# Layer A of a two-layer decoder step: scores by groups of chunks, odd units' scores and substitution beside the running chain

## The chip, the cores and the metric

One core of one Trainium2 chip runs the whole step as one program. The metric is device microseconds of one execution, the median of several. Five engines work side by side, each through its own list of instructions in a fixed order: PE (matmuls), DVE and ACT (elementwise work), POOL (a little elementwise work) and SP (which issues the DMAs). An instruction that waits holds up everything behind it on its engine.

## The reference, cut to what matters

Layer 0 is RWKV-7 time mixing over 272 prompt positions (16 meta tokens and 256 prompt tokens), 64 heads of 64; layer 1 is sliding-window attention. The change touches the recurrence of layer 0:

```python
def rwkv7_step(S, inp):
    r, d, k, v, kk, b = inp
    sa = jnp.einsum('bhij,bhj->bhi', S, kk)
    S = S * d[:, :, None, :] - sa[..., None] * b[:, :, None, :] + v[..., None] * k[:, :, None, :]
    return S, jnp.einsum('bhij,bhj->bhi', S, r)
...
rkvz = jnp.einsum('btpd,pde->btpe', xm[:, :, :4], w_rkvz)
S_fin, y = lax.scan(rwkv7_step, S0.astype(f32), (tm(r_h), tm(d_h), tm(k_h), tm(v_h), tm(kk), tm(b_h)))
...
return y @ w_out, S_fin.astype(S0.dtype), xn[:, -1]
```

## The kernel before, in words

**Big products.** Every large product is made with weights split into a high and a low part: `wunits` (L200) loads 256 KB of weights as one unit, ACT casts the high part `whi` (L195), DVE subtracts to get the low part `wlo` (L197), and PE makes three matmuls for each (L218 to L220). The pool that holds `raw`, `whi` and `wlo` has 5 buffers of each, so the split of unit u+5 can begin only when PE is done with unit u. A unit is 12 matmuls in two pieces of 6; the name of a unit ends with its place along the contraction, in steps of 2 (`wlo_v_1536_0`, `wlo_v_1536_2` follow each other, and after `_14` comes `_0` of the next column block).

**Phase A.** `drive` (L611) runs the products of layer 0 as the backbone: one piece per turn, counted by `self.pos`, and between pieces it lets generators ("streams") write their own instructions. A stream's `yield n, need` says: not before n more pieces, and not before the condition `need`. `after(n, *ks)` is the condition that the marks ks were set at least n pieces ago. PE's order is exactly the order in which this is written. DVE's and ACT's order is made by a scheduler by priority and expected times; the streams in `now` (epilogues and main) are written without a tie to the weights, main with a priority raised by 2000, and all others are tied behind the last split but one.

**The recurrence.** Heads go in 16 units u of four heads, in pairs o of an even and an odd unit. A unit is prepared by `prep` (decays, normalised keys) and `prep_e` (the tiles `KB`, keys times decay, and `E`, scored operands, one tile for all 272 positions). `scores` (L1000) then makes, by chunks of 64 positions (four, and one of 16), the products between positions (L1017, L1031), masks them back into `E` (L1024, L1025, L1037, L1038), and at its end transposes the keys to `BK` (L1049). After the odd unit's scores, `substitute` (L1054) inverts small triangular blocks on DVE: a transpose `NL` (L1069), 14 steps of two instructions (L1075, L1077), and the transposes `TN` and `TR` (L1081, L1082). `solve` (L1092) puts the blocks together on PE: `ps_so` (L1102) reads `TN`, and three more rounds follow (L1108, L1120, L1129). `chain` (L1170) then walks the five chunks; each step is three groups of matmuls (L1191, L1205 with L1208, L1214 with L1217) with copies on ACT and DVE between them, spaced 5, 2 and 3 pieces. `group_norm` (L1257) normalises and turns the result back (`ps_yt`, L1275).

In `main` these follow each other for each pair: chain of o, then scores of the next odd unit, substitution, solve of o+1, chain of o+1. The even unit's scores run beside the chain as a side stream. From the turn in which `substitute` is written to the first `ps_so` there are 3 and 3 pieces of the transposes and then 24 (27 from the sixth pair on): 30 or 33 pieces.

Of the kernel before, what the change touches and what calls it, by code (L numbers as in the profile page):

```python
# [109 lines left out]
class Kernel:  # L110
# [467 lines left out]
    def phase_a(self):  # L578
# [15 lines left out]
        for a in (self.KB, self.F, self.N16, self.Noff, self.Y):  # L594
# [9 lines left out]
        self.drive(self.products(), [self.epilogues(), self.main(), preps, self.decodes(), self.late_gates(), self.keep_r()],  # L604
                   {preps: [wait, need]})
# [4 lines left out]
    def drive(self, products, streams, begun, ahead=2000):  # L610
# [3 lines left out]
        now = streams[:2]  # L614
# [49 lines left out]
    def main(self):  # L664
        for o in range(-1, NU // 2):
            n = 2 * o + 2
            if o >= 0:
                yield from self.chain(o)
                self.mark('u', o)
                self.side.append(self.group_norm(o))  # L670
            if n < NU:
                yield 0, self.after(0, ('p', n + 1), ('c', n))
                self.side.append(self.load_x(o + 1))
                self.prep_e(n + 1)
                self.mark('e', n + 1)
                yield from self.scores(n + 1)
                yield from self.solve(o + 1)

                self.samples = True
                self.mark('s', o + 1)  # L680

    def preps(self):
        for n in range(NU):
            if n % 2 == 0 and n:
                yield 0, self.after(0, ('e', n - 1))
# [4 lines left out]
            if n % 2 == 0:  # L690

                self.prep_e(n)
                self.side.append(self.even_scores(n))

    def even_scores(self, n):
        if n:
            yield 0, self.after(0, ('s', n // 2 - 1))
        yield from self.scores(n)
# [159 lines left out]
    def prep(self, u):  # L858
# [31 lines left out]
        kT = w("kT", 2)  # L890
# [34 lines left out]
        if u >= 4:  # L925
            yield 0, self.after(0, ('g', u // 2 - 2))
        vT = w("vT", 4)
        dma(vT, self.vd[b][:, sl])

        sm = rp.tile([128, 2, 6, NS], F32, tag="sm", name=f"sm{u}")  # L930
        for i, x in enumerate((kk, a, kT, rT, vT, Pp[:, :, 5:])):
# [16 lines left out]
        for j in range(2):  # L948
            rk_of(j)
        for j in range(2):  # L950
# [8 lines left out]
    def prep_e(self, u):  # L959

        nc, rp = self.nc, self.rp
        V, A, G = nc.vector, nc.scalar, nc.gpsimd
        tt = V.tensor_tensor
        MU = ALU.mult
        kT, rT, kk, a, cl = (self.U[u][n] for n in ('kT', 'rT', 'kk', 'a', 'cl'))
        Pp = self.Pp
        ch = lambda x: x[:, :, :256].rearrange("p q (c t) -> p q c t", t=64)
        pch = Pp[:, :, :260].rearrange("p q (c t) -> p q c t", t=65)
# [5 lines left out]
        A.copy(KB[64:128, :, :, 128:192], KB[64:128, :, :, 0:64])  # L974

        E = rp.tile([128, 5, 2, L], F32, tag="E", bufs=3, name=f"E_{u}")
        tt(ch(E[:, 0]), ch(kk), pch[:, :, :, 0:64], op=MU)
        tt(ch(E[:, 2]), ch(rT), pch[:, :, :, 1:65], op=MU)
        tt(E[:, 0, :, 256:272], kk[:, :, 256:272], Pp[:, :, 260:276], op=MU)
        tt(E[:, 2, :, 256:272], rT[:, :, 256:272], Pp[:, :, 261:277], op=MU)  # L980
        A.copy(E[64:128, 1], E[64:128, 0])
        self.U[u]['E'] = E

    def scores(self, u):
        nc, rp = self.nc, self.rp

        odd = u % 2
        gap = iter((8, 3, 4, 3, 3) if odd else (8, 6, 6, 5, 4))
        turn = iter((0, odd, 0, odd, 0))
        def banks(nm):  # L990
            if next(turn):
                two = self.two_banks(f"ps_{nm[0]}{nm[1]}")
                return [two[:, q] for q in range(2)]
            return [self.bank(self.pe, f"ps_{nm[0]}{q}{nm[1]}") for q in range(2)]
        V, A, G = nc.vector, nc.scalar, nc.gpsimd
        tt = V.tensor_tensor
        MU = ALU.mult
        KB, E = self.KB, self.U[u]['E']
        i0 = 8 * (u % 2)
        H = lambda q: slice(64 * q, 64 * q + 64)  # L1000
        BK = rp.tile([128, 2, 5, 128], F32, tag="BK", bufs=3, name=f"BK{u}")
        self.U[u].update(BK=BK)

        rows = lambda q, j, a, b: E[H(q), q:3:2 - q, j, a:b]
        inst = lambda a, r, cs: a[r, i0:i0 + 8].rearrange("p (a c) t -> p a c t", c=4)[:, :, cs]
        bc = lambda m, *s: m.unsqueeze(1).unsqueeze(1).to_broadcast(s)
        for c0 in (0, 2):
            cs = slice(c0, c0 + 2)
            yield next(gap)
            ps = [b.rearrange("p (a c t) -> p a c t", a=2, c=2) for b in banks(("sc", f"{c0}_{u}"))]  # L1010

            with self.pe_order():
                for j in range(2):
                    for c in range(2):
                        for q in (1, 0):
                            o = 64 * (c0 + c)
                            nc.tensor.matmul(ps[q][:, j, c], KB[H(q), j, c0 + c, 64 * q:64 * q + 128],  # L1017
                                             rows(q, j, o, o + 64), start=True, stop=True)
            for q in range(2):
                pv, kr = ps[q], H(1 - q)  # L1020
                out = lambda i, r: E[r, i, :, 64 * c0:64 * c0 + 128].rearrange("p a (c t) -> p a c t", c=2)
                for r, a, t0 in ((64 * q, self.F, 0), (64 * q + 32, self.ND, 32)):
                    A.copy(inst(a, slice(r ^ 64 * odd, (r ^ 64 * odd) + 32), cs), pv[r:r + 32, :, :, t0:64])
                tt(out(q, kr), pv[kr, :, :, 0:64], bc(self.cst(C_MASK, 64, kr), 64, 2, 2, 64), op=MU)  # L1024
                tt(out(3 + q, slice(0, 128)), pv[:, :, :, 64:128], bc(self.cst(C_MASK + 64, 64), 128, 2, 2, 64), op=MU)  # L1025
        yield next(gap)
        ps = [b[:, :64].rearrange("p (a h t) -> p a h t", a=2, h=2) for b in banks(("sc", f"4_{u}"))]
# [945 lines left out]
```

## Time and profile before

| What | Value |
|---|---|
| Median of 3 runs | 2115.6 us (2114.31 to 2118.69) |
| The profiled execution | 2118.32 us |
| Its span in the trace | 2116.5 us |
| Granted TensorE clock, mean | 0.99 |
| PE, DVE, ACT, POOL busy, share of the span | 98%, 80%, 60%, 6% |
| DMA | 446.28 MB, 211 GB/s over the span |

The profiled execution is 2.7 us above the median of the runs, and 1.8 us of it lie outside the span. A busy share of PE counts a matmul to its modelled end, so that PE is shown idle only where the next instruction came later than that. In views of waits, "PE ps_so L1102 <- DVE TN L1081" says that PE's instruction of line 1102 started when DVE had finished line 1081.

### The profile page before, as it was taken

Reading aid. Unit: us, or ns where it says so; the run is one execution under the profiler, and the core shown is the slowest. Engines: PE = TensorE matmul, PEld = TensorE weight load, DVE = VectorE, ACT = ScalarE, POOL = GpSimd, SP = SyncE. Lnnn points to the kernel's source line nnn. Section 1 sums busy time; section 2 is a strip of 40 time slices with the busy share of each in tenths; the row PEclk is TensorE's granted clock in tenths of the full one; section 3 lists DMA queues with packets and bytes.
Section 4 is the critical chain, followed back from the end, with each engine's and each line's share of the span. In section 5 each row is a group of like instructions: output and inputs, shape, how many; then the busy total and the mean of one; then the engine's idle time right before and its main releaser. Section 6 shows DMA issues by size and latency. Waiting matters only on the chain.

```text
span 2116.5 us, 55871 instructions
## 1 busy us (share of the span) xinstructions
PE 2064.9 (98%) x21420; PEld 1965.8 (93%) x21420; DVE 1697.8 (80%) x4112; ACT 1263.8 (60%) x2790; POOL 122.5 (6%) x188
## 2 busy tenths in 40 slices
PE   9999999899999999999999999999999999999997
PEld 7999899889899989899999999999999999999997
DVE  8867777687678878888888788997888888878885
ACT  3457766576766757767676445565565655544443
POOL 0011100001010010100100001100000000000000
PEclk9999999999999999999999999999999999999999
DMA  7898667658756876777657687757455444567774
GB/s 258 314 312 250 189 213 241 188 181 290 216 180 205 260 229 198 211 217 222 203 152 246 207 257 243 247 172 227 132 167 156 146 155 130 181 210 247 232 219 132
DMA packets 276356, 446.28 MB, mean 211 GB/s; under 512 B 54056, under 2 KB 97768, under 8 KB 275696
## 3 DMA queue, kind: packets, MB, share of 16 engines
q1 hardware_dynamic: 275656, 441.66, 66.6%
q8 instruction: 168, 2.75, 0.5%
q10 hardware_dynamic: 432, 1.05, 0.1%
q14 instruction: 100, 0.82, 0.1%
HBM read 381.69 MB, written 65.03 MB: 211 GB/s over the span
## 4 chain that ended last, share of the span: by engine, by line
PE 87%; DVE 5%; ACT 3%; DMA 3%; issue 2%; SPq 0%; POOL 0%; DVEq 0%; POOLq 0%; ACTq 0%
PE ps_z L218 6%; PE ps_z L219 6%; PE ps_z L220 6%; PE ps_k L218 3%; PE ps_ob L218 3%; PE ps_ob L220 3%; PE ps_v L218 3%; PE ps_ob L219 3%; PE ps_r L218 3%; PE ps_q L218 3%; PE ps_q L220 3%; PE ps_q L219 3%; PE ps_k L219 3%; PE ps_k L220 3%; PE ps_v L220 3%; PE ps_v L219 3%
## 5 line engine op out<-in xcount | busy, mean ns | idle before, releaser
L218 PE MATMUL ps_z<-mhlm,whi_z 128*128 128x280 f32 x512 | 158.6, 310 | 2.8 <-ACT sr L937 2.0
L219 PE MATMUL ps_z<-mhlm,whi_z 128*128 128x280 f32 x512 | 150.6, 294 | 0.0
L220 PE MATMUL ps_z<-mhlm,wlo_z 128*128 128x280 f32 x512 | 150.3, 294 | 0.0
L218 PE MATMUL ps_q<-bmh,whi_qb 128*128 128x264 f32 x512 | 150.0, 293 | 0.1
L218 PE MATMUL ps_z<-bmh,whi_zb 128*128 128x264 f32 x512 | 147.4, 288 | 0.0
L220 PE MATMUL ps_q<-bmh,wlo_qb 128*128 128x264 f32 x512 | 145.6, 284 | 0.6 <-DVE wlo_qb L197 0.6
L219 PE MATMUL ps_q<-bml,whi_qb 128*128 128x264 f32 x512 | 145.6, 284 | 0.0
L219 PE MATMUL ps_z<-bml,whi_zb 128*128 128x264 f32 x512 | 145.5, 284 | 0.0
L220 PE MATMUL ps_z<-bmh,wlo_zb 128*128 128x264 f32 x512 | 145.4, 284 | 0.0
L218 PE MATMUL ps_ob<-ghi,whi_ob 128*128 128x264 f32 x512 | 145.3, 285 | 0.0
L220 PE MATMUL ps_ob<-ghi,wlo_ob 128*128 128x264 f32 x512 | 144.6, 284 | 0.0
L219 PE MATMUL ps_ob<-glo,whi_ob 128*128 128x264 f32 x512 | 144.6, 283 | 0.0
L195 ACT CAST whi_ob<-raw_ob 128x512 fp32r<-128x512 f32 x128 | 79.1, 620 | 96.9 <-PE ps_ob L219 77.8
L195 ACT CAST whi_oa<-raw_oa 128x512 fp32r<-128x512 f32 x128 | 79.2, 620 | 88.0 <-PE ps_oa L219 30.6
L197 DVE TENSOR_TENSOR wlo_r<-raw_r,whi_r 128x512 fp32r<-128x512 f32 x128 | 87.8, 691 | 42.6 <-ACT whi_r L195 41.3
L218 PE MATMUL ps_v<-mhlm,whi_v 128*128 128x280 f32 x384 | 119.8, 312 | 0.4 <-ACT st L790 0.4
L218 PE MATMUL ps_k<-mhlm,whi_k 128*128 128x280 f32 x384 | 119.1, 310 | 1.0 <-ACT st L790 1.0
L195 ACT CAST whi_v<-raw_v 128x512 fp32r<-128x512 f32 x128 | 79.0, 619 | 65.8 <-PE ps_v L219 37.7
L197 DVE TENSOR_TENSOR wlo_v<-raw_v,whi_v 128x512 fp32r<-128x512 f32 x128 | 87.3, 687 | 36.9 <-ACT whi_v L195 35.6
L195 ACT CAST whi_zb<-raw_zb 128x512 fp32r<-128x512 f32 x128 | 78.2, 619 | 62.9 <-PE ps_z L219 38.5
L220 PE MATMUL ps_k<-mhlm,wlo_k 128*128 128x280 f32 x384 | 112.4, 293 | 2.1 <-issue 2.1
L219 PE MATMUL ps_v<-mhlm,whi_v 128*128 128x280 f32 x384 | 112.7, 293 | 0.0
(478 smaller groups left out, 7604.1 us busy)
## 6 DMA issues: line engine op xcount, KB each, us to landing
raw_k<-a_w_rkvz SPq DMA_DIRECT2D x128, 256.0 KB
raw_v<-a_w_rkvz SPq DMA_DIRECT2D x128, 256.0 KB
raw_r<-a_w_rkvz SPq DMA_DIRECT2D x128, 256.0 KB
raw_z<-a_w_rkvz SPq DMA_DIRECT2D x128, 256.0 KB
raw_oa<-a_w_out SPq DMA_DIRECT2D x128, 256.0 KB
raw_qb<-b_w_qz SPq DMA_DIRECT2D x128, 256.0 KB
raw_zb<-b_w_qz SPq DMA_DIRECT2D x128, 256.0 KB
raw_ob<-b_w_o SPq DMA_DIRECT2D x128, 256.0 KB
```

The source lines that it names most:

```text
L195: self.nc.scalar.copy(hi, src)
L197: return self.nc.vector.tensor_tensor(lo, src, hi.bitcast(F32), op=ALU.subtract)
L218: mm(ps, wh, xh, start=start, stop=False)
L219: mm(ps, wh, xl, start=False, stop=False)
L220: return mm(ps, wl, xh, start=False, stop=stop)
```

## The change

Scored operands are kept as three tiles for each unit (`E0` for chunks 0 and 1, `E1` for 2 and 3, `E2` for the last 16 positions) and the transposed keys as two (`BK0` for chunks 0 and 1, `BK1` for the rest). `prep_e` is cut into `prep_k` (the keys) and two parts; `scores` makes one group of chunks at a call; `turns` makes the transposes, those of chunks 0 and 1 together with the scores of the last chunk in one PSUM bank. `substitute` is cut into `strict` (its POOL part) and the rest, which uses `TN` as scratch in place of `stmp`. A new stream `odds` does the odd unit's work of pair o as soon as the chain of o-1 has finished chunk 1 (marks `k`), and `main` holds only chain and solve: the solve comes 24 pieces after the mark `t`, which is set where `substitute` is written. `odds` is in `now` but main alone keeps the raised priority. A chain step is spaced 6, 3 and 4 pieces. The four `TT` activations move from `substitute` into `solve`, behind the first `ps_so`. The chain's last chunk reads 64 columns of `E` where it read 16, and its memset and one copy of `W` are gone. `vT` is loaded later, `kT` has one buffer in place of two.

```diff
-        self.drive(self.products(), [self.epilogues(), self.main(), preps, self.decodes(), self.late_gates(), self.keep_r()],
-                   {preps: [wait, need]})
+        self.drive(self.products(), [self.epilogues(), self.main(), self.odds(), preps, self.decodes(), self.late_gates(),
+                                     self.keep_r()], {preps: [wait, need]}, now=3)
...
-        now = streams[:2]
+        now = streams[:now]
...
     def main(self):
         for o in range(-1, NU // 2):
-            n = 2 * o + 2
             if o >= 0:
                 yield from self.chain(o)
                 self.mark('u', o)
                 self.side.append(self.group_norm(o))
-            if n < NU:
-                yield 0, self.after(0, ('p', n + 1), ('c', n))
+            if 2 * o + 2 < NU:
                 self.side.append(self.load_x(o + 1))
-                self.prep_e(n + 1)
-                self.mark('e', n + 1)
-                yield from self.scores(n + 1)
+                yield 0, self.after(24, ('t', o + 1))
                 yield from self.solve(o + 1)
...
+    def odds(self):
+        for o in range(NU // 2):
+            u = 2 * o + 1
+            step = lambda c: [('k', o - 1, c)] if o else []
+            yield 0, self.after(0, ('p', u), ('c', u - 1), *step(1))
+            self.prep_k(u)
+            self.mark('b', u)
+            self.prep_e(u, 0)
+            yield 8
+            self.scores(u, 0)
+            yield 6
+            self.scores(u, 4)
+            yield 5, self.after(1, *step(3))
+            self.prep_e(u, 1)
+            self.mark('e', u)
+            yield 6
+            self.scores(u, 2)
+            self.strict(o)
+            yield 6
+            self.substitute(o)
+            self.mark('t', o)
+            yield 4, self.after(0, *([('u', o - 1)] if o else []))
+            self.turns(u, 1)
+            self.mark('c', u)
...
-        yield 24 if o < 5 else 27
+        TT = self.TT = rp.tile([128, 20, 64], F32, tag="TT", name=f"TT{o}")
         ps = self.bank(self.pe, f"ps_so{o}")
...
         ET = ev("ET", 16, 16)
         V.tensor_copy(ET, ps[:, 0:256].rearrange("p (i s) -> p i s", s=16))
+        for b in range(4):
+            A.activation(TT[:, :, 16 * b:16 * b + 16], TR[:, :, 0:20].rearrange("p t i -> p i t"), AF.Copy,
+                         scale=self.cst(C_M64 + 16 * b, 1))
...
-            yield (5 if c else 3), (None if c or not o else self.after(2, ('g', o - 1)))
+            yield (6 if c else 3), (None if c or not o else self.after(2, ('g', o - 1)))
...
-            yield 2
+            yield 3
...
-            yield 3
+            yield 4
...
-            yield 3 if j else 36 if o < NU // 2 - 1 else 19
+            yield 3 if j else 24 if o < NU // 2 - 1 else 19
```

What the change does to the order shows best where the second pair (o = 1) is solved. First DVE before; `NL1` and `stmp1` are the substitution's tiles, `wlo_v_1280_14` is the last unit of a column block and `wlo_v_1536_0` the first of the next:

```order
L1077 TENSOR_TENSOR NL1_5077<-NL1_5077,stmp1_14_5118 128x2x14
L197 TENSOR_TENSOR wlo_v_1280_14_5425<-raw_v_1280_14_5422,whi_v_1280_14_5424 128x512
L904 TENSOR_TENSOR kT4_5445<-kT4_5445,km1_4_5457 128x280
L906 TENSOR_TENSOR ta4_4872<-ta4_4872,kk4_5449 128x560
L1081 STREAM_TRANSPOSE TN1_5123<-NL1_5077 128x512
L1082 STREAM_TRANSPOSE TR1_5124<-NL1_5077 128x512
L1276 SCALAR_TENSOR_TENSOR vT0_2043<-ps_yt0_0_5399,par_79,vT0_2043 128x272
L197 TENSOR_TENSOR wlo_v_1536_0_5475<-raw_v_1536_0_5472,whi_v_1536_0_5474 128x512
```

`TN1` stands behind the split of unit `v_1280_14`. The same place on DVE now:

```order
L197 TENSOR_TENSOR wlo_v_1536_10_5665<-raw_v_1536_10_5662,whi_v_1536_10_5664 128x512
L974 SCALAR_TENSOR_TENSOR rk0_4_5775<-rT4_5452,par_79,kT4_5450 128x272
L974 SCALAR_TENSOR_TENSOR rk1_4_5779<-rT4_5452,par_79,kT4_5450 128x272
L1123 TENSOR_TENSOR TN1_5188<-NL1_5187 128x52
L1127 MEMSET NL1_5187 128x16 x2
L197 TENSOR_TENSOR rkllo4_5774<-rk0_4_5775,rklhi4_5773 128x272
L1125 TENSOR_TENSOR NL1_5187<-NL1_5187,TN1_5188 128x4x13
L197 TENSOR_TENSOR rkllo4_5774<-rk1_4_5779,rklhi4_5773 128x272
L1123 TENSOR_TENSOR TN1_5188<-NL1_5187 128x28
L1125 TENSOR_TENSOR NL1_5187<-NL1_5187,TN1_5188 128x2x14
L1128 STREAM_TRANSPOSE TN1_5188<-NL1_5187 128x512
L1129 STREAM_TRANSPOSE TR1_5189<-NL1_5187 128x512
```

`TN1` has moved behind the split of unit `v_1536_10`, and work of another unit (`rk`, `rkllo`) stands between the last steps of the substitution. On PE, the place of the first `ps_so1` before:

```order
L218 MATMUL ps_v_1280_1_5310<-mhlm2_11_7_5014,whi_v_1280_14_5424 128x280
L219 MATMUL ps_v_1280_1_5310<-mhlm2_11_7_5014,whi_v_1280_14_5424 128x280
L220 MATMUL ps_v_1280_1_5310<-mhlm2_11_7_5014,wlo_v_1280_14_5425 128x280
L218 MATMUL ps_v_1536_0_5518<-mhlm2_11_0_4747,whi_v_1536_0_5474 128x280
L219 MATMUL ps_v_1536_0_5518<-mhlm2_11_0_4747,whi_v_1536_0_5474 128x280
L220 MATMUL ps_v_1536_0_5518<-mhlm2_11_0_4747,wlo_v_1536_0_5475 128x280
L218 MATMUL ps_v_1536_0_5518<-mhlm2_11_0_4747,whi_v_1536_0_5474 128x280
L219 MATMUL ps_v_1536_0_5518<-mhlm2_11_0_4747,whi_v_1536_0_5474 128x280
L220 MATMUL ps_v_1536_0_5518<-mhlm2_11_0_4747,wlo_v_1536_0_5475 128x280
L1102 MATMUL ps_so1_5538<-TN1_5123,Noff_1742 32x16 x64
```

and now:

```order
L218 MATMUL ps_v_1536_1_5514<-mhlm2_11_0_4700,whi_v_1536_0_5440 128x280
L219 MATMUL ps_v_1536_1_5514<-mhlm2_11_0_4700,whi_v_1536_0_5440 128x280
L220 MATMUL ps_v_1536_1_5514<-mhlm2_11_0_4700,wlo_v_1536_0_5441 128x280
L218 MATMUL ps_v_1536_0_5513<-mhlm2_11_1_4718,whi_v_1536_2_5492 128x280
L219 MATMUL ps_v_1536_0_5513<-mhlm2_11_1_4718,whi_v_1536_2_5492 128x280
L220 MATMUL ps_v_1536_0_5513<-mhlm2_11_1_4718,wlo_v_1536_2_5493 128x280
L218 MATMUL ps_v_1536_0_5513<-mhlm2_11_1_4718,whi_v_1536_2_5492 128x280
L219 MATMUL ps_v_1536_0_5513<-mhlm2_11_1_4718,whi_v_1536_2_5492 128x280
L220 MATMUL ps_v_1536_0_5513<-mhlm2_11_1_4718,wlo_v_1536_2_5493 128x280
L883 MATMUL ps_vt10_0_5545<-consts_78,st2_10_5502 128x128 x2
L883 MATMUL ps_vt10_0_5545<-consts_78,st2_10_5502 16x128
L1145 MATMUL ps_so1_5552<-TN1_5188,Noff_1742 32x16 x64
```

Before, PE reached `ps_so1` in unit `v_1536_0`, one unit past the split in front of `TN1`. Now it reaches it in unit `v_1536_2`, four units short of the split in front of `TN1`, with 6 matmuls of a product and 3 transposes since the end of unit `v_1536_0`.

The same counts for all eight pairs, from the two orders: by how many units the last split in front of `TN` is ahead of the unit in which PE reaches the first `ps_so`; for the changed kernel also how many instructions DVE has from that split to `TN`, both included, and how many matmuls of products PE has from the end of the unit whose buffer that split takes to `ps_so`.

| Pair o | 0 | 1 | 2 | 3 | 4 | 5 | 6 | 7 |
|---|---|---|---|---|---|---|---|---|
| units ahead, before | 4 | -1 | 1 | 1 | 0 | 5 | 1 | -1 |
| units ahead, now | 4 | 4 | 3 | 4 | 4 | 4 | 4 | 3 |
| DVE instructions, now | 8 | 12 | 8 | 17 | 13 | 31 | 23 | 3 |
| matmuls between, now | 6 | 6 | 22 | 6 | 6 | 6 | 6 | 18 |

Three more counts from the orders. In phase A the places where PE has something else between two products were 368 and are 348. The first `kk` that is built from the second group's key norms (`kk4`) stood 4 weight splits behind the last step of those norms on DVE and now stands 7 behind. The last `ps_yt` of phase A stood 23 pieces ahead of the products' end and now stands 54 ahead.

More of the change, by code (lines that the diff above doesn't have):

```diff
@@ L974, in prep_e @@
         A.copy(KB[64:128, :, :, 128:192], KB[64:128, :, :, 0:64])
[L976 to L980, printed above, removed]
-        A.copy(E[64:128, 1], E[64:128, 0])
[L982 to L998, printed above, removed]
+        self.U[u]['E'], self.U[u]['BK'] = {}, {}
@@ L1019, in scores @@
             for q in range(2):
                 pv, kr = ps[q], H(1 - q)
[L1021 to L1025, printed above, removed]
@@ L1194, in chain @@
             W2 = W.rearrange("p (f k) i -> p f (k i)", f=2)
-            if c < 4:
-                A.copy(W2, part(0, slice(0, 128)))
-            else:
-                G.memset(W, 0.0)
-                for q in range(2):
-                    A.copy(W2[R(q)], part(0, R(q)))
-            yield 2
+            A.copy(W2, part(0, slice(0, 128)))
+            yield 3
             with self.pe_order():
```

194 lines of the change are left out of this document (121 added, 73 removed).

## The prediction, on record before the run

> **What bounds the kernel now.** I read the page's busy times first, then a table of busy times by stage, then the waits of PE in the stage that the change touches, then the timeline around the two largest of them.
>
> ```profile
> PE 2064.9 (98%) x21420; PEld 1965.8 (93%) x21420; DVE 1697.8 (80%) x4112; ACT 1263.8 (60%) x2790; POOL 122.5 (6%) x188
> ```
>
> PE bounds the whole. The table has, for a stretch in us, its length, then busy time (and instructions) of PE, PEld, DVE, ACT and POOL, then PE's granted clock, DMA share and GB/s; phase A is the first row.
>
> ```profile
> 200.00:1215.00 1015.00, 983.92 (x12721) 922.45 (x12719) 806.41 (x1834) 682.32 (x1523) 79.04 (x124) 0.98 0.69 214
> 1215.00:2000.00 785.00, 782.38 (x6554) 764.91 (x6553) 659.98 (x1816) 430.47 (x978) 23.49 (x28) 1.00 0.63 193
> ```
>
> PE idles 1015.00 - 983.92 = 31.1 us in phase A and 2.6 behind it. So nothing but phase A can give or take time, and that the last chain now ends earlier is worth nothing by itself. The largest waits there (us in total, times, longest):
>
> ```profile
> PE ps_yt L1275 <- DVE vT L1276: 8.0, 2, 6.9
> PE ps_so L1102 <- DVE TN L1081: 6.1, 2, 3.5
> ...
> PE ps_z L218 <- ACT sr L937: 2.0, 1, 2.0
> ```
>
> The second row is the solve waiting for the substitution: two of eight solves. This is the first of them, pair 0 (start, duration):
>
> ```profile
> 252.14 0.69 DVE L197 TENSOR_TENSOR wlo_r<-raw_r,whi_r 128x512 fp32r<-128x512 f32 x1 [0.17 <-ACT whi_r L195]
> 252.46 0.29 PE L220 MATMUL ps_r<-mhld,wlo_r 128*128 128x280 f32 x1
> 252.75 0.92 DVE L898 SCALAR_TENSOR_TENSOR kk<-kT,par,kk 128x280 f32<-128x280 f32 x2
> 253.69 1.33 DVE L910 TENSOR_TENSOR_SCAN cl<-reset,cl 128x272 f32<-128x272 f32 x2
> 255.14 1.05 DVE L1081 STREAM_TRANSPOSE TN<-NL 128x512 f32<-128x512 f32 x1
> 256.24 0.44 PE L1102 MATMUL ps_so<-TN,Noff 32*32 32x16 f32 x31 [3.50 <-DVE TN L1081]
> ```
>
> And pair 5:
>
> ```profile
> 911.42 0.69 DVE L197 TENSOR_TENSOR wlo_z<-raw_z,whi_z 128x512 fp32r<-128x512 f32 x1
> 912.03 0.18 DVE L1077 TENSOR_TENSOR NL<-NL,stmp 128x28 f32<-128x28 f32 x1
> 912.25 1.04 DVE L1081 STREAM_TRANSPOSE TN<-NL 128x512 f32<-128x512 f32 x1
> 913.43 0.78 PE L1102 MATMUL ps_so<-TN,Noff 32*32 32x16 f32 x43 [2.56 <-DVE TN L1081]
> ```
>
> DVE had no way to be earlier: the split in front of TN waits for a buffer that PE frees only at the end of the unit before the one in which it reaches the solve, since the buffers are five deep and the split is 4 (pair 0) and 5 (pair 5) units ahead. PE then runs out of work while DVE goes from that split to TN. In the other six pairs the split is at most one unit ahead, and none of them waits. Let S be the sum of DVE's work from that split to TN, both included. For pair 0 it is 4.6 (the rows shown and two small steps between them) and the wait 3.50, with 9 matmuls between freed buffer and solve; for pair 5 it is 2.0 and the wait 2.56, with none. So a wait is S - 1.1 with nine matmuls and S + 0.6 with none; for six, in proportion, S - 0.5.
>
> **The change, part by part.** *The solve's wait.* Now that split is 3 or 4 units ahead in every pair: the lag from the substitution to the solve is 24 pieces instead of 30 or 33, and the substitution's steps, without main's priority, are mixed with other DVE work. The durations (group, count, busy us, mean ns, idle before):
>
> ```profile
> L197 DVE TENSOR_TENSOR wlo_v<-raw_v,whi_v 128x512 fp32r<-128x512 f32 x96 | 65.5, 687 | 29.7 <-ACT whi_v L195 28.4 <-DMA vt<-vk 0.8
> L794 DVE SCALAR_TENSOR_TENSOR st<-th,st 128x280 f32<-128x280 f32 x32 | 14.2, 443 | 1.0 <-ACT th L793 1.0
> L945 DVE SCALAR_TENSOR_TENSOR rk<-rT,par,kT 128x272 f32<-128x272 f32 x29 | 13.3, 495 | 0.0
> L1266 DVE TENSOR_TENSOR Y<-Y,gvar 128x1536 f32<-128x1536 f32 x7 | 12.3, 1751 | 0.1
> L197 DVE TENSOR_TENSOR rkllo<-rk,rklhi 128x272 fp32r<-128x272 f32 x30 | 12.2, 433 | 0.5 <-ACT rklhi L195 0.4
> L1081 DVE STREAM_TRANSPOSE TN<-NL 128x512 f32<-128x512 f32 x8 | 8.8, 1096 | 0.1
> L806 DVE SCALAR_TENSOR_TENSOR st<-st,yl 128x544 f32<-128x544 f32 x12 | 8.6, 718 | 0.0
> L1077 DVE TENSOR_TENSOR NL<-NL,stmp 128x88 f32<-128x88 f32 x16 | 4.0, 248 | 0.3
> L1077 DVE TENSOR_TENSOR NL<-NL,stmp 128x28 f32<-128x28 f32 x16 | 3.1, 192 | 0.2
> ```
>
> Pair 1 has 12 instructions: split 0.69, two `rk` 0.99, two `rkllo` 0.87, four last steps 0.8, two memsets 0.15 (estimated under the smallest step), TN 1.10: S = 4.6, wait 4.1. Pair 5 has 31: split 0.69, one instruction like L794 0.44, two like L806 1.44, `Y` 1.75, seventeen steps of the substitution at 0.25 4.2, TN 1.10, and eight small ones at 0.1 to 0.19 each: S = 10.4 to 11.1, taken 10.8, wait 10.3. By the same rows pairs 0, 3, 4 and 6 have S = 4.4, 5.5, 4.0 and 8.5, waits 3.9, 5.0, 3.5, 8.0. Pairs 2 and 7 have S = 2.7 and 2.0 and some twenty matmuls between: 0.4 and 0.2. Together 35.4 where 6.1 stands now: +29.3. Bounds: with 0.6 more or less for each of the six, +25.5 to +33.
>
> *The clock behind a wait.* Stretches behind the waits at 256, 382, 913 and 1049 us:
>
> ```profile
> 257.50:260.90 3.40, 3.40 (x16) 3.40 (x16) 0.87 (x2) 2.92 (x5) 0.00 (x0) 0.50 0.22 33
> 382.00:387.10 5.10, 5.10 (x23) 5.09 (x24) 2.21 (x4) 3.44 (x6) 0.00 (x0) 0.50 0.49 165
> 913.50:919.60 6.10, 6.10 (x146) 6.03 (x147) 1.26 (x3) 3.96 (x6) 0.20 (x1) 0.50 0.85 278
> 1049.40:1052.70 3.30, 3.30 (x16) 3.30 (x15) 2.79 (x7) 1.09 (x2) 0.00 (x0) 0.50 0.55 153
> ```
>
> PE ran at half clock for 3.3 to 6.1 us, so each cost half of that: 1.7, 2.6, 3.1 and 1.6. The two behind `ps_so` cost 4.8 now. Six waits of 3.5 us or more at 2.5 each make 15: +10.2, between 6 x 1.6 - 4.8 = +4.8 and 6 x 3.1 - 4.8 = +13.8. The Trainium skill ("TensorE: Matmul & The Clock Gate", Part 1: The HAM clock gate) lets the clock fall only after an idle window of about 3.4 us; the rows show half clock also behind 2.56 and 2.0 us, so the trace differs. By that rule the same six waits count and the two small ones don't, so that the sum would hardly move.
>
> *The key norms.* The 6.9 us wait at `ps_yt` comes from DVE, which stood still for this:
>
> ```profile
> 375.65 0.51 DVE L898 SCALAR_TENSOR_TENSOR kk<-kT,par,kk 128x280 f32<-128x280 f32 x1 [4.24 <-DMA kk<-kr]
> ```
>
> That `kk` now stands seven splits behind the norms where it stood four. PE needs a new split every 12 matmuls, and matmuls follow each other 0.13 us apart (below), 1.55 us a unit: three more units are 4.65, over 4.24. So 6.9 and its 2.6 of clock go: -9.5, or nothing if the load starts later by as much.
>
> *Other waits.* 31.1 - 6.1 - 6.9 = 18.1 us of idle time in many waits of 2 us and less, and three stretches of half clock (the one at 1049 among them) of 1.6 each: 22.9. The chain's steps are 13 pieces where they were 10, so their products wait less often, and every wait for TN lets DVE and ACT catch up. I let half go, -11.4; the ends are 0 and -22.9.
>
> *Changes between products and other matmuls.* 20 fewer.
>
> ```profile
> 536.51 0.29 PE L220 MATMUL ps_k<-mhlm,wlo_k 128*128 128x280 f32 x1
> 536.74 1.20 PE L1120 MATMUL ps_so<-TN,F 32*32 32x32 f32 x64
> ...
> 537.87 0.40 PE L218 MATMUL ps_k<-mhlm,whi_k 128*128 128x280 f32 x1
> 538.10 0.29 PE L219 MATMUL ps_k<-mhlm,whi_k 128*128 128x280 f32 x1
> 538.23 0.29 PE L220 MATMUL ps_k<-mhlm,wlo_k 128*128 128x280 f32 x1
> ```
>
> Going in takes 0.23 where products follow each other after 0.13, and so does coming back: 0.2 each, -4 (0 if the groups joined paid nothing).
>
> *The last chunk* reads 64 columns where it read 16:
>
> ```profile
> L1191 PE MATMUL ps_ch<-X,E 128*64 128x64 f32 x368 | 16.3, 229 | 1.4 <-DVE X L1227 1.1 <-ACT X L1227 0.2
> L1191 PE MATMUL ps_ch<-X,E 128*16 128x64 f32 x112 | 4.4, 220 | 0.0
> ```
>
> 112 x 9 ns = +1.0. The memset and the copy that go, the group cuts of `E`, and the four `TT` activations behind the first `ps_so` are taken at nothing: DVE and ACT are idle for 209 and 333 us of phase A, and pieces of products lie between the solve's rounds. If that cover is gone they show as a wait at the solve's later rounds.
>
> Sum: +29.3 +10.2 -9.5 -11.4 -4.0 +1.0 = +15.6. On the profiled execution 2118.3 + 15.6 = 2133.9; that execution is 2.7 above the median, so 2131 us (+0.7%).
>
> **The rivals.**
> (a) *The waits for TN grow.* A stall of PE holds back the buffers, and through them SP's loads; in before's order DVE once stood 4.24 us for a `kk` load, and builds of `kk` stand close to the solves of pairs 3, 4 and 6 now. With `kT` in one buffer, a load that comes later would fall into S itself. Three such waits are 3 x 4.24 = 12.7 more, with `ps_yt` kept 9.5: 2144 to 2153. For it: PE has no store of splits there. Against: only one such wait in the whole trace.
> (b) *It balances.* All other waits go (-11.4 more) and the solves' are at their lower bounds (-3.8): +0.4, 2116, within 0.2%, which is about what a measurement of this kernel can tell from no change.
> (c) *Faster.* The spacing of 13 pieces and odd work beside the chain take all other waits away: -9.5 - 22.9 - 4 + 1 = -35.4. It decides where the waits for TN with their clock stay under 35.4 + 6.1 + 4.8 = 46.3, against 50.4 in my sum. If they come to half, 17.7 with three falls of the clock at 2.5, it is +11.6 + 2.7 - 35.4 = -21, 2094.5. For it: most of the waits in the table name DVE or ACT as releaser, work that another spacing of the chain moves. Against: the order is fixed, and the counts of units leave DVE no way to run ahead of the buffers. The Trainium skill ("Perfetto Trace Analysis", Optimization Strategy) expects interleaving of stages with different limits to help; here PE is 97% busy in the stage itself, so the trace leaves that rule 31.1 us to win.
> (d) *It doesn't do what it says*: the solves would be as early as before. The order shows them moved, so no chance of its own.
>
> **How the numbers follow.** Forecast 0.62, (a) 0.16, (b) 0.10, (c) 0.12. Slower by over 0.2% (above 2119.8): forecast and (a), 0.78. Within: 0.10. Faster (below 2111.4): 0.12. The range: downward all other waits gone and the solves' waits 4 to 5 us less, 2131 - 11.4 - 4.6 = 2115; upward none of them gone and the two bounds of waits and clock, 2131 + 11.4 + 3.7 + 3.6 = 2150, taken 2151. Outside are (c) and half of (a).
>
> **What would show it.** In the changed profile: PE `ps_so` L1145 waiting for TN L1128 about 35 us in six to eight waits, the longest near 10 in pair 5; half clock behind six of them; no wait of 6.9 at `ps_yt`; phase A's idle time near 45 us. Wrong is it if the waits for TN stay under 15 us, or a load is named ahead of them, or the other waits don't shrink.

## The result, and the profile after

The changed kernel takes 2167.4 us (2163.4 to 2170.2) against 2117.1 us (2114.3 to 2118.9) for the kernel before: ratio 1.0237, 95% interval 1.0215 to 1.0259. Slower was forecast, but by 15.6 us; measured are 50.2, and the time lies above the range of 2115 to 2151. The two profiled executions have spans of 2116.5 and 2167.0 us, 50.5 apart, and the readings below account for those 50.5. In them "lag" is the distance in pieces from the place where `substitute` is written to the solve, and "waits for TN" are PE's waits at the first `ps_so` of a pair.

The page's busy times of the changed kernel:

```profile
PE 2072.1 (96%) x21420; PEld 1974.8 (91%) x21420; DVE 1701.0 (78%) x4144; ACT 1264.0 (58%) x2814; POOL 118.8 (5%) x164
```

PE has 7.2 us more of busy time with the same count of matmuls, so that most of the loss is idle time. One stretch holds all the idle time that changes: 200 to 1290 us, before and now (columns as in the prediction: length, then PE, PEld, DVE, ACT, POOL, granted clock, DMA share, GB/s).

```profile
200.00:1290.00 1090.00, 1058.87 (x13415) 995.54 (x13414) 867.74 (x1965) 720.00 (x1588) 79.56 (x126) 0.99 0.69 216
```

```profile
200.00:1290.00 1090.00, 1015.63 (x13016) 955.09 (x13015) 843.56 (x1950) 700.85 (x1576) 76.89 (x105) 0.96 0.66 207
```

Idle time of PE: 31.1 us before, 74.4 now, +43.3. PE's largest waits in that stretch of the changed kernel, and below them the third kind of wait at the chain's products:

```profile
PE ps_so L1145 <- DVE TN L1128: 44.1, 8, 13.1
PE ps_yt L1322 <- DVE Y L1313: 4.9, 1, 4.9
PE ps_sm L964 <- POOL sm L961: 4.8, 2, 4.2
PE ps_ch L1242 <- ACT X L1273: 4.1, 1, 4.1
PE ps_ch L1242 <- DVE X L1273: 2.9, 3, 1.6
...
PE ps_ch L1251 <- ACT W L1246: 1.0, 1, 1.0
```

The waits at the chain's products (`ps_ch`) in the kernel before:

```profile
PE ps_ch L1205 <- ACT W L1196: 1.3, 2, 0.9
PE ps_ch L1191 <- DVE X L1227: 1.1, 1, 1.1
PE ps_ch L1214 <- ACT X L1210: 1.1, 2, 0.9
...
PE ps_ch L1191 <- ACT X L1227: 0.2, 1, 0.2
```

They came to 3.7 us before and come to 8.0 now, although the chain's steps are spaced wider.

The first row of the changed kernel is the one that was forecast: all eight solves now wait for the substitution, 44.1 us where 6.1 stood. The waits of the six pairs that were to wait are 3.8, 4.6, 6.6, 4.5, 13.1 and 10.2 us in pairs 0, 1, 3, 4, 5 and 6; forecast were 3.9, 4.1, 5.0, 3.5, 10.3 and 8.0. This is the worst of them, pair 5 (start, duration):

```profile
910.63 0.29 PE L220 MATMUL ps_z<-mhlm,wlo_z 128*128 128x280 f32 x1
911.02 0.62 ACT L195 CAST whi_z<-raw_z 128x512 fp32r<-128x512 f32 x1 [3.17 <-DMA raw_z<-a_w_rkvz]
911.67 0.69 DVE L197 TENSOR_TENSOR wlo_z<-raw_z,whi_z 128x512 fp32r<-128x512 f32 x1 [3.29 <-ACT whi_z L195]
...
914.11 0.69 DVE L197 TENSOR_TENSOR wlo_z<-raw_z,whi_z 128x512 fp32r<-128x512 f32 x1
...
917.90 1.75 DVE L1313 TENSOR_TENSOR Y<-Y,gvar 128x1536 f32<-128x1536 f32 x1
...
922.82 1.04 DVE L1128 STREAM_TRANSPOSE TN<-NL 128x512 f32<-128x512 f32 x1
...
924.00 1.20 PE L1145 MATMUL ps_so<-TN,Noff 32*32 32x16 f32 x74 [13.09 <-DVE TN L1128]
```

PE's last product ends at 910.9. The split in front of TN starts only at 914.11: DVE had first stood 3.29 us for a weight unit that ACT could not cast because its load had not landed. From that split to the end of TN it takes 9.7 us (10.8 was the sum of its parts; instructions on DVE overlap a little), with the large `Y` of the group norm in the middle. Late split and work behind it are 3.2 + 9.7 = 12.9 of the 13.1.

The clock falls behind each long wait. Four stretches, the first and second behind the waits of pairs 5 and 6, the third behind that of pair 0, the last behind a wait of 1.6 us at a chain step:

```profile
914.50:931.60 17.10, 7.60 (x153) 7.58 (x154) 13.19 (x39) 6.19 (x10) 0.20 (x1) 0.50 0.35 108
1051.00:1064.60 13.60, 6.52 (x148) 6.50 (x149) 8.75 (x25) 3.73 (x6) 3.06 (x2) 0.50 0.23 83
266.00:269.40 3.40, 3.40 (x16) 3.40 (x16) 0.96 (x2) 3.04 (x5) 0.00 (x0) 0.50 0.65 195
1115.90:1119.30 3.40, 3.40 (x19) 3.14 (x21) 2.51 (x5) 1.25 (x2) 0.00 (x0) 0.50 0.70 235
```

Half of PE's busy time in such a stretch is counted as lost: 3.8, 3.3, 1.7 and 1.7 us here. (That is a little high: in the last stretch products start 0.23 us apart, at 1116.25, 1116.49 and 1116.72, where they start 0.13 apart at full clock, so 44% is lost.) Over all stretches at half clock between 200 and 1290 us it is 26.3 us, where it was 12.6 before: +13.7. So 43.3 of idle time and 13.7 of clock, less a remainder of 6.5, make the 50.5. Of the remainder 1.7 is a stretch of 3.4 us at half clock that the kernel before has at 1390.7 us, outside the table, and the changed kernel does not have; some 4.8 are left as saved in PE's work.

The other waits did not shrink. Beside TN, PE idles 30.3 us now; before it was 25.0, of which the 6.9 at the first transposes back are gone, as forecast. Three new waits make 13.2 us of it. The first:

```profile
581.60 0.18 DVE L295 TENSOR_SCALAR rsyk<-kx 128x35 int32<-128x35 int32 x1 [5.92 <-DMA kx<-kr]
...
591.22 0.47 PE L1242 MATMUL ps_ch<-X,E 128*64 128x64 f32 x2 [4.12 <-ACT X L1273]
```

DVE stands 5.92 us for the key norms' load itself (3.2 was the longest such wait before), and then works without a pause up to the steps that the chain's `X` needs; the chain step comes 4.1 us late. The second, on POOL and PE:

```profile
1017.44 1.11 POOL L1106 TENSOR_TENSOR nd<-F,consts 128x320 f32<-128x320 f32 x1
1018.50 1.06 POOL L1107 TENSOR_TENSOR nd<-F,consts 128x320 f32<-128x320 f32 x1
1019.52 0.72 POOL L1109 TENSOR_TENSOR Noff<-F,consts 128x256 f32<-128x256 f32 x1
1020.18 0.19 POOL L961 COPY sm<-ta 128x16 f32<-128x16 f32 x1
```

```profile
1020.43 0.45 PE L964 MATMUL ps_sm<-consts,sm 128*96 128x128 f32 x1 [4.17 <-POOL sm L961]
```

The odd unit's masking on POOL (`strict`) has come in front of a small copy of another unit's preparation, which waits 2.8 us behind it and PE with it; the rest of the 4.2 is DVE, which has the copy's source ready only at 1017.4. The third is the `ps_yt` row of 4.9 us above: the last pair's group norm now ends beside the gates of the next stage, and its steps on DVE stand between theirs.

### The profile page after: what moved, and what is told of

It reads as the page before. It is cut to its first block, busy times and chain, and to the rows that moved or that the text cites. A ratio compares the mean times of both kernels' runs of the same rounds, so it can differ in the third digit from the quotient of the medians.

```text
span 2167.0 us, 55914 instructions
## 1 busy us (share of the span) xinstructions
PE 2072.1 (96%) x21420; PEld 1974.8 (91%) x21420; DVE 1701.0 (78%) x4144; ACT 1264.0 (58%) x2814; POOL 118.8 (5%) x164
## 4 chain that ended last, share of the span: by engine, by line
PE 82%; DVE 9%; DMA 4%; ACT 2%; issue 2%; POOL 0%; SPq 0%; DVEq 0%; POOLq 0%; ACTq 0%
PE ps_z L218 6%; PE ps_z L219 6%; PE ps_z L220 6%; PE ps_ob L220 3%; PE ps_ob L218 3%; PE ps_ob L219 3%; PE ps_q L218 3%; PE ps_q L220 3%; PE ps_q L219 3%; PE ps_v L218 3%; PE ps_v L220 2%; PE ps_v L219 2%; PE ps_r L218 2%; PE ps_k L218 2%; PE ps_r L219 2%
## 5 line engine op out<-in xcount | busy, mean ns | idle before, releaser
L197 DVE TENSOR_TENSOR wlo_oa<-raw_oa,whi_oa 128x512 fp32r<-128x512 f32 x128 | 87.7, 690 | 42.3 <-ACT whi_oa L195 40.7
L218 PE MATMUL ps_k<-mhlm,whi_k 128*128 128x280 f32 x384 | 118.4, 308 | 0.6 <-ACT st L821 0.6
L219 PE MATMUL ps_k<-mhlm,whi_k 128*128 128x280 f32 x384 | 112.6, 293 | 0.0
```

Source lines behind the costliest of these rows:

```text
L197: return self.nc.vector.tensor_tensor(lo, src, hi.bitcast(F32), op=ALU.subtract)
L218: mm(ps, wh, xh, start=start, stop=False)
L219: mm(ps, wh, xl, start=False, stop=False)
```

## The experiments

All are compared with the kernel before on the same chip. The theories: **lag**, the waits for TN follow from the lag between substitution and solve and from the fixed order of DVE; **load**, DVE carries too much beside the chain and is late whatever the lag. Idle, TN and clock in the table are PE's idle time between 200 and 1290 us, the part of it at the first `ps_so` for TN, and the time lost at half clock, each from the profiled execution. "Light" kernels leave out a part of the decode work on DVE; "odd work behind" means that the odd unit's work follows the chain again.

| Kernel | us | ratio to before (95%) | idle | TN | other idle | clock |
|---|---|---|---|---|---|---|
| before | 2117.1 | | 31.1 | 6.1 | 25.0 | 12.6 |
| changed | 2167.4 | 1.0237 (1.0215 to 1.0259) | 74.4 | 44.1 | 30.3 | 26.3 |
| e1 lag 30 | 2148.7 | 1.0133 (1.0116 to 1.0150) | 56.8 | 9.6 | 47.2 | 20.9 |
| e2 before, lag cut | 2142.3 | 1.0108 (1.0093 to 1.0123) | 49.0 | 16.1 | 32.9 | 23.1 |
| e3 spacing, lag 33 | 2137.6 | 1.0088 (1.0068 to 1.0107) | 47.4 | 4.4 | 43.0 | 19.6 |
| e4 raised priority | 2167.1 | (one run) | 72.4 | 44.0 | 28.4 | 24.7 |
| e5 odd work behind | 2133.4 | 1.0073 (1.0048 to 1.0099) | 43.9 | 12.2 | 31.7 | 13.9 |
| e6 changed, light | 2151.2 | 1.0158 (1.0135 to 1.0181) | 63.4 | 42.9 | 20.5 | 20.9 |
| e7 lag 30, light | 2140.1 | 1.0098 (1.0069 to 1.0126) | 52.1 | 10.4 | 41.7 | 20.0 |
| e8 before, light | 2114.4 | 0.9983 (0.9968 to 0.9998) | 30.0 | 6.2 | 23.8 | 13.5 |
| e9 before, longer lag in two pairs | 2105.1 | 0.9940 (0.9922 to 0.9957) | 22.6 | 0.0 | 22.6 | 9.6 |
| e10 as e9, preparation later | 2109.6 | 0.9959 (0.9943 to 0.9975) | 27.9 | 0.0 | 27.9 | 6.3 |
| e11 as e5, longer lag in two pairs | 2134.9 | 1.0061 (1.0040 to 1.0083) | 39.0 | 3.9 | 35.1 | 20.7 |
| e12 lag 30, group norm 36 | 2144.1 | 1.0119 (1.0098 to 1.0140) | 54.9 | 24.1 | 30.8 | 16.8 |
| e13 as e9, four small edits | 2112.2 | 0.9977 (0.9964 to 0.9990) | 30.4 | 3.8 | 26.6 | 9.3 |
| e14 as e9, group norm 24 | 2111.4 | 0.9964 (0.9951 to 0.9977) | 33.0 | 4.8 | 28.1 | 10.9 |
| e15 as e11, group norm 36 | 2129.7 | 1.0064 (1.0043 to 1.0085) | 42.8 | 1.7 | 41.1 | 6.1 |

**e1, the lag put back to 30 pieces.**

```diff
-                yield 0, self.after(24, ('t', o + 1))
+                yield 0, self.after(30, ('t', o + 1))
```

> The changed kernel with the solve 30 pieces behind the substitution in place of 24, all else kept. Lag theory: the lag alone makes the waits for TN. In this order the split in front of TN is still 4 units ahead in pairs 3, 5 and 6, with 2 to 4 us of DVE work behind it, so 2 to 3 us of wait each there and little elsewhere: TN waits fall from 44.1 to 5 to 10 us, the clock loss from 26 to about 17, and the time from 2167 to 2115 to 2130. Load theory: DVE is late because it now carries the odd unit's scores beside the chain, whatever the lag; then TN waits stay above 25 us and the time above 2145.

PE's waits in this kernel, the first five:

```profile
PE ps_so L1145 <- DVE TN L1128: 9.6, 3, 4.2
PE ps_yt L1322 <- DVE Y L1313: 9.0, 2, 5.4
PE ps_so L1154 <- issue: 6.0, 3, 3.8
PE ps_o L218 <- DVE xr L816: 5.6, 1, 5.6
PE ps_ch L1242 <- ACT X L1273: 2.5, 1, 2.5
```

The waits for TN are at 9.6 us in three pairs, as the lag theory said. The time is not: 2148.7 where 2115 to 2130 was expected. Of 34.5 us taken away at the solve, 16.9 came back in other waits (30.3 to 47.2). The load theory, which wanted TN waits above 25, is wrong on them but right that the time stays above 2145.

**e2, the lag cut in the kernel before.**

```diff
-        yield 24 if o < 5 else 27
+        yield 18 if o < 5 else 21
```

> The kernel before with the lag of the substitution to the solve cut by 6 pieces (24 to 18, 27 to 21), no interleaving. Lag theory: the split in front of TN comes to stand 2 to 5 units ahead; by S - 0.5 with six matmuls between and S + 0.6 with none that is about 4 us in pair 0, 2.6 in pair 5, 2.9 in pair 6 and 1 or less elsewhere, 8 to 12 us where the kernel before has 6.1; with the clock +5 to +10 us in all, 2122 to 2127. Load theory: no interleaving, so no more waits than before: TN waits near 6 and the time within 4 us of 2117.

```profile
PE ps_so L1102 <- DVE TN L1081: 16.1, 6, 5.3
```

Six solves wait, 16.1 us (8 to 12 were expected), without any interleaving: six pieces of lag decide. The size was too small again, 2142.3 where 2122 to 2127 was expected: other waits grew by 7.9 us and the loss of clock by 10.5.

**e4, the lost priority.**

```diff
-                            with self.tc.high_priority(offset=ahead if s[0] is now[1] else 0), turn:
+                            with self.tc.high_priority(offset=ahead if s[0] in now[1:] else 0), turn:
```

> The changed kernel with the raised priority for the odd units' stream as well as for main. The prediction named the lost priority as one of two reasons for the mixed substitution. If that is so, TN waits fall clearly below 44 us; if the lag alone decides, the order of DVE and with it time (2163 to 2171) and TN waits (43 to 45) stay.

2167.1 us in its one run, and the row reads as without it:

```profile
PE ps_so L1145 <- DVE TN L1128: 44.0, 8, 13.0
```

The count of DVE instructions from the split in front of TN to TN is also the same in all eight pairs. The priority that the odd units lost has no part in it.

**e6, e7 and e8, less work for DVE.** In all three the decode recurrence leaves out 62 of 64 columns of its products with the state:

```diff
-                tt(T, S, rowb(w), op=MU)
-                V.reduce_sum(o[:, iq], T, axis=AX.X)
+                tt(T[:, :, :2], S[:, :, :2], rowb(w)[:, :, :2], op=MU)
+                V.reduce_sum(o[:, iq], T[:, :, :2], axis=AX.X)
```

> The changed kernel, with 62 of the 64 columns of the decode recurrence's two products and sums over the state left out (some 120 instructions of 0.69 us on DVE become short ones of under 0.15: 65 to 75 us of DVE work less, loads kept); the DVE order in front of TN stays as it is. Lag theory for TN: the waits for TN keep what follows from the order, 35 of 44 us, and lose only the 8 us by which DVE was late; time down by 10 to 20. Load theory: all waits go with DVE's load, TN below 20, time down by 40 or more.

> The same piece of the decode left out of the kernel with the lag of 30. If what is left there over the kernel before (29 us) is DVE's load beside the chain, most of it goes: 2148.7 down to 2115 to 2125, the waits other than TN from 47 to under 30. If it is fixed order (POOL, the group norm ahead, code and loads), time falls by less than 10.

> The same piece of the decode left out of the kernel before, as the measure for the other two: before waits 31 us in phase A, and DVE is idle for a fifth of it, so the load theory has it fall by 5 to 10 us and the changed kernel by far more; if the load acts on both alike, it falls as much as the others.

The stretch of 200 to 1290 us and the first row of the waits in e6:

```profile
200.00:1290.00 1090.00, 1026.64 (x13152) 967.05 (x13151) 795.22 (x1964) 707.74 (x1587) 80.71 (x105) 0.97 0.67 210
```

```profile
PE ps_so L1145 <- DVE TN L1128: 42.9, 8, 12.0
```

DVE has 48 us less to do there (843.6 to 795.2; 57 over the whole program, where 65 to 75 were expected), and the waits for TN hardly move, 44.1 to 42.9, where 35 were expected. They come from the order of the instructions, not from how busy DVE is; even the late splits stay. What the load makes is in the other waits, 30.3 to 20.5, and in the clock. The times fall by 16 us in the changed kernel, by 8.6 with the lag at 30 (under the 10 of fixed order; its other waits stay at 41.7) and by 3.7 in the kernel before (5 to 10 were expected). So of the 29 us over the kernel before that were left with the lag at 30, some 5 are load by this measure (8.6 less 3.7). By the ratios the 8.6 are 7 us with an interval of 7 to either side, so these 5 are not clear of noise.

**e3 and e5, the spacing of the chain and the place of the odd work.** e3 has chain steps of 5, 2 and 3 pieces and a lag of 33. e5 has, beside that, the odd unit's work behind the chain:

```diff
-            yield 0, self.after(0, ('p', u), ('c', u - 1), *step(1))
+            yield 0, self.after(0, ('p', u), ('c', u - 1), *([('u', o - 1)] if o else []))
...
-            yield 5, self.after(1, *step(3))
+            yield 3
```

> The changed kernel with the chain's steps spaced 5, 2 and 3 pieces as before, and the solve 33 pieces behind the substitution. Lag theory: the split in front of TN is at most 2 units ahead but in pairs 3 and 6; TN waits about 3 to 5 us in all. What then stays over the kernel before is the interleaving itself: other waits 20 to 30 us (18.1 before and 6.9 at the transposes back), so 2105 to 2125. Load theory: closer steps leave DVE less time for each, so waits inside the chain steps (ps_ch) grow from 9 us to over 20 and the time stays above 2140.

> The changed kernel with the odd unit's work put back behind the chain (it starts when the chain of the pair before has ended, with 3 pieces between its parts), chain steps of 5, 2 and 3 pieces and a lag of 33: the same pace as the kernel before (112 to 116 pieces a pair), but with all of the change's tiles, groups, moved copies and loads. If the place of the odd unit's work beside the chain makes the waits that are left at a lag of 30 (47 us beside those for TN), they fall to about 25 and the time comes to 2110 to 2125. If the other edits make them (one kT buffer, the late vT load, the POOL part cut off, the group norm 24 pieces ahead), the time stays above 2135.

e3 brought the waits for TN to 4.4 us and left 43.0 of others, so it fell neither into the one range nor above the other; waits at the chain's products were 9.2 us. In e5 the others fell to 31.7 and the loss of clock to 13.9, waits for TN came back in two pairs (12.2), and the time of 2133.4 is between the two ranges. e3 and e5 differ only in the place of the odd work and the distance between its parts: 1.0088 and 1.0073, which cannot be told apart. So at a lag of 33 the place moves waits from one row to another, and no cost of interleaving by itself is clear of noise. From e1 to e3 (1.0133 to 1.0088, about 10 us) the chain's spacing and three pieces of lag change together; which of them gives the 10 us was not tried.

**e9 and e10, the kernel before with a longer lag where it waited.**

```diff
-        yield 24 if o < 5 else 27
+        yield 24 + 6 * (o in (0, 5)) + 3 * (o >= 5)
```

> The kernel before with 6 more pieces between substitution and solve in pairs 0 and 5 alone, the two that wait for TN. The split in front of TN is then at most 2 units ahead with 36 matmuls or more between, in every pair. Lag theory: the 6.1 us of waits for TN and the 4.8 us of half clock behind them go, time 2118 to 2105 to 2111, faster than both kernels. Rival: the wait moves to the next stage, since DVE and ACT lose the rest that the wait gave them; then within 4 us of 2118.

```profile
200.00:1290.00 1090.00, 1067.44 (x13498) 1003.68 (x13497) 879.80 (x1983) 723.96 (x1598) 81.69 (x128) 0.99 0.70 219
```

The group of the first `ps_so` in this kernel (busy, mean ns, idle before):

```profile
L1102 PE MATMUL ps_so<-TN,Noff 32*32 32x16 f32 x1024 | 10.2, 184 | 0.0
```

No solve waits for TN any more, and the kernel is faster than both, 2105.1 us, at the lower end of what was expected. This is the mechanism of the prediction in the other direction.

e10 adds `self.after(14, ('n', u // 4), ...)` for 6 in `prep`.

> The same, and a unit from the second group on is prepared 14 pieces behind the mark of its key norms in place of 6. Then DVE reaches the first kk that waits for the norms later, its 4.24 us of standing still go and with it the 6.9 us at the first transposes back and 2.6 us of clock: 8 to 10 us below the run with pairs 0 and 5 alone, 2096 to 2103. Rival: the rest of the preparation comes too late for what follows and the wait returns there: no gain.

2109.6 us, ratio 0.9959 (0.9943 to 0.9975): no gain on top, where 2096 to 2103 was expected. The wait at the first transposes back was already down to 1.0 us in e9: with `kk` in its old place, DVE stood only 0.58 us for its load there, not 4.24.

**e11, the same cure for the changed kernel behind the chain.** As e5, with the lag at 39 for the two chains whose next solves had waited most.

> The changed kernel with the odd unit's work behind the chain again and a lag of 33, now 39 for pairs 4 and 5 counted from the chain before (the two solves that waited 6.4 and 5.8 us). If the lag is what was left, the 12 us for TN and 5.7 of clock go: 2133 down to 2112 to 2120, level with the kernel before, so that tiles, groups, moved copies and loads cost nothing. If the new tiles and queues cost something of their own, it stays above 2124.

```profile
200.00:1290.00 1090.00, 1051.04 (x13273) 987.72 (x13272) 862.97 (x1976) 713.47 (x1597) 72.36 (x105) 0.98 0.68 213
```

TN waits fell from 12.2 to 3.9 us, but the time did not: 2134.9, with 35.1 of other waits and 20.7 of lost clock. Expected was 2112 to 2120 if only the lag were left, and it was not.

**e12, the group norm's lag.** `yield 3 if j else 36` in place of 24, with the lag at 30.

> The changed kernel with a lag of 30 and with 36 pieces in place of 24 ahead of the first transposes back of each pair's group norm, as before the change. The two waits for Y (9.0 us, with some 3.6 of clock) go. But DVE's steps behind the split in front of TN grow in pairs 5 and 6 from 3.2 and 1.6 us to 5.6 and 5.0, so 5 to 6 us come back at the solve: 2148.7 to 2140 to 2148. A fall of more than 12 us would show the short lag of the group norm as a main cause of what is left.

```profile
PE ps_so L1145 <- DVE TN L1128: 24.1, 4, 9.5
```

The waits for `Y` are gone and the ones for TN are back, 24.1 us. Behind the split the work is as expected, 5.6 and 5.2 us in pairs 5 and 6. But the split itself starts 3.5 and 4.1 us after PE has stopped, and the group norm's steps stand in front of it. In pair 6:

```profile
1042.84 1.74 DVE L1313 TENSOR_TENSOR Y<-Y,gvar 128x1536 f32<-128x1536 f32 x1
...
1047.35 0.68 DVE L197 TENSOR_TENSOR wlo_z<-raw_z,whi_z 128x512 fp32r<-128x512 f32 x1
```

PE's last product ends at 1043.3. 2144.1 us, ratio 1.0119 (1.0098 to 1.0140): as expected in time, with a larger exchange than the 5 to 6 us expected.

**e13 to e15, what is left.** e13 puts four small edits of the change into e9; e14 the last of them alone; e15 takes the group norm's lag back in e11.

```diff
-        kT = w("kT", 2)
+        kT = w("kT")
...
-            tmp = rp.tile([128, 112], F32, tag="stmp", name=f"stmp{o}_{s}")
...
-            yield 3 if j else 36 if o < NU // 2 - 1 else 19
+            yield 3 if j else 24 if o < NU // 2 - 1 else 19
```

> The kernel before with the longer lag in pairs 0 and 5, and four of the change's small edits: one kT buffer in place of two, TN as scratch for the substitution, the four TT activations behind the first ps_so, the first transposes back 24 pieces behind the group norm in place of 36. Still open is why the changed kernel keeps 30 us over this one when its odd work is put back behind the chain and its lag is long. If the small edits make that, this run loses most of it: over 2120. If not, it stays within 6 us of 2105, and the cost lies in the groups of scored operands and transposed keys and what they reorder.

> The same kernel with the last of the four edits alone: 24 pieces in place of 36 ahead of the first transposes back. If the short lag of the group norm costs, waits at ps_yt rise from 2.8 us towards the 9.0 that the changed kernel with a lag of 30 showed, and time to 2110 or more; if it costs only where the odd work lies beside the chain, time stays within 4 us of 2105.

> The changed kernel with the odd unit's work behind the chain, lag 33 and 39, and 36 pieces ahead of the transposes back again: everything of the order is then as before, only the groups, the buffers and loads are the change's. If the group norm's lag was the rest, 2135 falls to 2115 or less; if the groups are, it stays above 2128.

e13 takes 2112.2 us, some 8 us above e9 by the ratios (0.9977 and 0.9940; the two intervals allow 3 to 12), between the two ranges that were expected. e14, with the group norm's lag alone, takes 2111.4 and cannot be told from e13. As expected for a lag that costs, it is above 2110, but the waits at `ps_yt` rise only from 2.8 to 5.6 us; the other 4.8 are waits for TN, which are back. e15 takes 2129.7, above 2128, as expected if the groups cost; it cannot be told from e11.

So the four small edits cost about 8 us. What the rest of the change costs shows between kernels with the same lag of the group norm: e11 and e13 have 24 pieces, 1.0061 - 0.9977 = 0.8%, about 18 us; e15 and e9 have 36, 1.0064 - 0.9940 = 1.2%, about 26 us, with the other three small edits in it (the lags of each two are close but not equal). It lies in what e11 and e15 still have of the change: scores by groups, the keys transposed in two parts, the POOL part cut off, the late load of `vT`, the last chunk. Which of these it is stays open. In e15 the longest single row of PE's waits is for `sm` on POOL, 7.6 us in 4, so the POOL queue is one candidate; that was not tried by itself.

## Why the prediction was wrong, point by point

**The waits for TN: the mechanism right, the size short.** +29.3 was forecast, +38.0 came. The working behind the split was right: in pairs 0, 1, 3, 4, 5 and 6 DVE took 3.7, 3.9, 4.9, 3.6, 9.7 and 7.8 us from the split to the end of TN, and 4.4, 4.6, 5.5, 4.0, 10.8 and 8.5 were added up. What was missed is the split itself: the rule "S - 0.5" lets it start the moment PE frees the buffer. It started 0.0, 0.6, 1.6, 0.8, 3.2 and 2.3 us after PE had stopped, 8.5 us in all. In pair 5 a late weight load did it, which is rival (a) with another load than the one named, and is also one of the prediction's own signs of being wrong. In pairs 1, 3, 4 and 6 DVE had no idle time right in front of the split: it was busy with what its order puts there. One of the two reasons given was wrong: the priority does nothing (e4), the lag does it (e1, e2, e9).

**Other waits: the step that failed.** "I let half go, -11.4; the ends are 0 and -22.9." They grew, which the prediction had named as a sign of being wrong. In idle time alone, 18.1 us of small waits, of which half was to go, became 30.3: +12.2 for -9.1, an error of 21 us out of 35. Three things were wrong with the step. The chain's wider steps were to make its products wait less often, and these waits rose from 3.7 to 8.0 us. The upper end was no change, though the change moved work past two queues in which others stand: POOL, which the prediction never counted, and the key norms on DVE, where it counted only that one wait of 4.24 us goes and not that a `kx` load is waited for as well. And the other reason given for the gain was that a wait for TN lets DVE and ACT catch up. e1 fits that: with most of the waits for TN taken away the others rose to 47.2. But then one wait is only the cover of another, and the solves' waits come on top. With less work on DVE (e6) the others fall from 30.3 to 20.5, so part of them is DVE's load, which the step left out; what makes each of the rest was traced for the three new waits alone.

**The clock.** +10.2 for the solves, less 2.6 and 2.4 for what was to go, is +5.2; it was +13.7. Six waits cost 18.7 us, 3.1 each, where 2.5 was taken; this is the upper bound that was given. The rest stands behind other waits, which were to shrink.

**The key norms.** Right in number: 6.9 us at the first transposes back are gone, and the 2.6 of clock with them. The reason is less sure. In e9 that `kk` stands four splits behind the norms, as before, and in e2 three, and DVE waits only 0.6 and 0.5 us for it; from the norms' last step to `kk` it is 9.3 us in the kernel before, 7.1 in e9 and 8.1 in e2. So the place alone did not make the wait; how long the load took had its part, and why it took longer there is open.

**Fewer changes between products and other matmuls, the last chunk.** -3.0 was forecast; PE's busy time less the lost clock gives -6.5, or some -4.8 without the stretch at 1390.7 us, an error on the good side.

The errors add up: 8.7 at the solve, 21.2 in other waits, 8.5 in the clock, -3.5 in PE's own work, 34.9 in all, which is 50.5 - 15.6.

**The rivals.** None came out. (a) wanted three solves to wait for `kk` loads, and the 6.9 us at `ps_yt` to stay or go, 2144 to 2153: no `kk` load was late at a solve's split, and the time is above that. (b) wanted all other waits gone. Nor (c), the faster kernel: the chain's wider steps did not take the other waits away. The sum of TN waits and their clock was far past the 46.3 us from which it would have decided.

## What to carry to other kernels

Where instruction orders are fixed and buffers are n deep, count for every hand-over how many units the producing engine's last split stands ahead of the consumer; here, with n = 5, what the producer did behind a split 4 units ahead became idle time for the consumer, and so did the lateness of that split (42.9 us of the 44.1, in six pairs), also with 57 us less work on the producer (e6); at 3 units ahead it was 0.9 and 0.3 us. A shorter lag costs at other places too (e2): bound the waits that a change does not touch from above as well, and list every in-order queue (POOL and the loads too) past which it moves work. The cheap gain was a few pieces more of lag at the two hand-overs that stood at the limit (e9: 0.6%, 0.4% to 0.8%).

## What the runs showed of the hardware that was not expected

The clock fell to 0.50 for 3.4 us behind a wait of only 1.6 us (at 1115.9, quoted above), and in the kernel before behind one of 1.23 us (wait to 665.87, half clock from 667.1). And PE sometimes stops inside a group of matmuls with nothing shown to wait for: in e1, after 126 of 128 equal ones,

```profile
1178.66 1.23 PE L1154 MATMUL ps_so<-TR,ET 32*16 32x16 f32 x126
1183.70 0.21 PE L1154 MATMUL ps_so<-TR,ET 32*16 32x16 f32 x2 [3.81 <-issue]
```

Such stops make 6.0 us there in that group and cannot be read from an order of instructions.
